# Delta rule of a hybrid block on one core: k-k and q-k products with 256 columns at a time, strictly alternating heads, and a later turn of nbp

## The chip, the cores and the metric

The kernel runs on one core of a Trainium2 chip. A core has five engines that run at the same time, each through its own instructions in order: TensorE (PE; its weight loads are shown apart as PEld), VectorE (DVE), ScalarE (ACT), GpSimd (POOL) and SyncE (SP), which here issues nearly all DMAs. The metric is the device time in microseconds of one execution; lower is better.

## The reference, cut to what matters

One block of a hybrid network on 1024 tokens of width 1024, in float32: a dilated attention of 8 heads and a gated delta rule of 8 heads side by side, their joint output projection, then a gated feed-forward part. The change touches the delta rule, which works in chunks:

```
q = l2norm(q) / sqrt(64); k = l2norm(k)            # per head, 64 wide
gcum   = cumsum(g) within a chunk
a_mat  = strictly_lower((beta * k) @ k.T * exp(gcum_i - gcum_j))
sol    = solve(a_mat + I, [beta * v, beta * k * exp(gcum)])   # u and w
qk     = lower(q @ k.T * exp(gcum_i - gcum_j))
for each chunk:                                     # the scan over the state
    v_new = u - w @ state
    o     = (q * exp(gcum)) @ state + qk @ v_new
    state = state * exp(g_last) + (k * exp(g_last - gcum)).T @ v_new
```

So each head needs, for every chunk, the products k @ k.T and q @ k.T, both multiplied with the same table of decays.

## The kernel before, in words

The kernel takes chunks of 128 positions, eight of them. The eight delta heads are worked through in two groups g of four heads (`delta(0)`, `delta(1)`); within a group, heads go in pairs q = 0, 1, and a pair's two heads lie in one tile, one head in partitions 0 to 63 and the other in 64 to 127. `kd[hp]` and `qd[hp]` are the k and q of pair hp = 2g + q, transposed (64 rows for each head, 1024 positions), each a tile of its own in the pools' tags "kd" and "qd" with two buffers each.

`delta` first makes k and q of a group by convolution (`conv`, for the second group in `delta_early` with a detour through memory: the DMA of L1240 brings it back from `_.cv`), and turns them (`delta_turn`, L737) for their norms. Then `delta_prep` does this:

- It makes the norms rk, and from them nbp (L774), nbg, kds and lr.
- ScalarE turns the tables `lts[h]` (named dt in the trace) into decays, one exponential for each head h and position block n (L770), head after head.
- `nbp` is transposed on the PE (L780, bank `ps_bp`), copied out, and written to memory (`bp_d`, L783), from where `delta_rows_in` reads it back in another layout (`bpr`, L855) for the inverse.
- For each pair: four q-k products for each head into one PSUM bank, then the other four; then the same for k-k (L799, tiles `kk_q` and `kk_k`). A product has 64 rows and 128 columns. DVE multiplies each full bank of 512 columns with the decays (L805): q-k into the tiles `qk`, k-k in place into `lts`. The k-k results go to memory (`lt_d`, L812).
- POOL scales kt with kds and qd with its own decays (L824, L839).

After that `delta_rows_in` loads the k-k results (`nt`, L853); `delta_inverse` multiplies them with bpr (L888), inverts 32 x 32 blocks in 31 steps on DVE (L899, L903), sends the result through memory (`tn`, L908) and joins the blocks for each head with PE products (the first of them at L931). `delta_scan` runs over the chunks; its readout uses qd (L1045).

Banks: `sbank` and `tbank` hand out two PSUM banks each, `abank` one. A tile that uses a bank again waits until its last reader is done.

The PE's other work in this phase is the projections (`others`, written as a generator through `proj_d`, L590, and `proj_t`, L616; their weights are split into a high and a low part by ACT and POOL, one of them by DVE, L230 and L231). They are put between the products of the delta rule by hand: `turn(name)` takes as many microseconds of them as the table `FILL` says for that name, and orders the instructions inside it behind the last of them. `tc.issue_after(ins)` orders what is written inside it behind `ins` on the same engine. `until` and `hold` take other products until one of them is done; `hold` stands ahead of the inverse's PE products, with 4 us for the first group and 24 for the second. What is left is spread over the first units of attention (`attend`, `FRONT - used[0]`). Every 7.6 us of other products, `modulation` adds a burst of its own (L211). Where no order is given, the framework takes instructions by priority, mostly in the order of the program.

Of the kernel before, what the change touches and what calls it, by code (L numbers as in the profile page):

```python
# [18 lines left out]
P = 128  # L19
# [33 lines left out]
    "S0_0_0": 3.84,  # L53
    "S1_0_0": 5.12,
    "trv2_0": 12.8,
    "kk1_0_0_q": 6.4,
    "trq1_0False": 4.48,
    "trk1_0False": 1.92,
    "kk0_2_0_k": 1.28,
    "lc0_0": 1.92,  # L60
    "trq3_0False": 2.56,
    "et0_0_0": 1.92,
    "sy1_6": 1.92,
    "kk1_3_0_k": 0.64,
    "et5_5_4": 1.28,
    "y0_0": 0.64,
    "trv3_0": 10.24,
    "kk1_0_0_k": 0.64,
    "sb0_6": 1.92,
    "et7_4_4": 0.64,  # L70
    "et4_6_0": 0.64,
# [1 line left out]
    "S6_0_0": 0.64,  # L73
    "sy1_0": 0.64,
    "sy1_7": 0.64,
    "kk0_0_0_k": 0.64,
}
for step in "abcd":
    for h in range(4):
        FILL.setdefault(f"l{step}0_{h}", 0.64)  # L80


def build(tc, I, out):
# [69 lines left out]
    def tbank(name):  # L153
        return psb(name, "t", 2)

    def abank(name):
        return psb(name, "a", 1)
# [4 lines left out]
    def start(name, tag, shape=None, dt=F32):  # L162

        n = {"xp": 2, "qk": 4, "lu": 5, "o": 2, "VN": 2, "R": 1, "tc": TCB, "yt": 1, "os": 1, "zl": 1}.get(tag, 2)
        return (pr if tag in ("dt", "xp") else pd).tile(shape or [P, T], dt, name=name, tag=tag, bufs=n)
# [7 lines left out]

    rb = const([33, 8], "rb")
    nc.vector.memset(rb[32:33, :], 1.0)
    tbl = start("tbl", "qd", [33, T]), start("tbl2", "qd", [33, P])
    wa8 = start("wa8", "qk", [P, KT, P])
    for i in range(2):
        nc.sync.dma_start(wa8[:, 4 * i : 4 * i + 4], I["wa8"][:, 4 * i : 4 * i + 4])
# [11 lines left out]
    for j in range(3):  # L191
# [5 lines left out]
        Rs = start(f"Rs{j}", "tc", [8, HALF])  # L197
        nc.vector.tensor_scalar(out=Rs[:, 0:n], in0=ps[:8, 0:n], scalar1=-1.0, scalar2=None, op0=ALU.mult)
        Rss.append(Rs)
    sqs = [start(f"sq{i}", "qd") for i in range(2)]  # L200

    sh1 = const([P, KT + 31], "sh1")
    nc.vector.memset(sh1, 0.0)
# [51 lines left out]
    wf = [start(f"wf{j}", ("dt", "xp")[j // 2], [P, 2, HALF]) for j in range(3)]  # L255
    wf = [wf[k // 2][:, k % 2] for k in range(5)]
    wf += [wp.tile([P, WSLOT], F32, name=f"wf{k}", tag="wr", bufs=3)[:, 0:HALF] for k in range(5, 8)]
    xts = [start(f"xt{k}", "lu" if k < 5 else ("vb" if k < 7 else "kd")) for k in range(KT)]

    def x_load(k):  # L260
        nc.sync.dma_start(xts[k], I["xT"][k * P : (k + 1) * P])
# [53 lines left out]
            )  # L315

    V0 = 16
    vraw = [start(f"vraw{i}", ("kd", "kt")[i], [P, 2, HALF]) for i in range(2)]

    def v_load(s):  # L320
        for j in range(2):
# [234 lines left out]
            )  # L556
        nc.scalar.activation(dst, dst, AF.Silu)

    kd, qd = {}, {}
    last, taken = [None], [None]  # L560
    fill = [None]
    used = [0.0]
# [1 line left out]
    def ahead(us):  # L564
# [7 lines left out]
            used[0] += w  # L572
        return some and last[0] is not None

    @contextmanager
    def turn(name):

        with tc.issue_after(last[0].ins) if ahead(FILL.get(name, 0)) else ExitStack():
            yield


# [171 lines left out]
    def delta_prep(g, st, norms, kt, lts):  # L753

        rk, eq, nbp, nbg, kds, lr = (norms[k] for k in ("rk", "eq", "nbp", "nbg", "kds", "lr"))
        gs = slice(32 * g, 32 * g + 32)

        def g3(t):
            return t[:, gs].rearrange("p (n h) -> p n h", n=8)

        eqf = eq.rearrange("p n h -> p (n h)")

        if g == 1:
            nc.scalar.activation(lr, rk, AF.Ln, bias=eps1)
        nc.vector.tensor_scalar(out=lr, in0=lr, scalar1=-0.5, scalar2=None, op0=ALU.mult)
        nc.scalar.activation(rk, lr, AF.Exp)
        nc.vector.tensor_tensor(out=lr, in0=lr, in1=g3(Gc), op=ALU.subtract)
        for h in range(4):
            for n in range(8):
                nc.scalar.activation(lts[h][:, n], lts[h][:, n], AF.Exp, bias=lr[:, n, h : h + 1])  # L770
        nc.vector.tensor_scalar(
            out=eqf, in0=eqf, scalar1=EPS, scalar2=64 * EPS, op0=ALU.add, op1=ALU.mult
        )
        nc.vector.scalar_tensor_tensor(  # L774
            out=nbp, in0=g3(beta), scalar=-1.0, in1=rk, op0=ALU.mult, op1=ALU.mult
        )
        nc.vector.tensor_tensor(out=nbg, in0=nbp, in1=g3(eG), op=ALU.mult)
        nc.vector.tensor_tensor(out=kds, in0=rk, in1=g3(edec), op=ALU.mult)
        ps = tbank(f"ps_bp{g}")
        nc.tensor.transpose(ps[:32, 0:P], nbp.rearrange("p n h -> p (n h)"), ident)  # L780
        nbpT = pd.tile([32, P], F32, name=f"nbpT{g}", tag="nbpT", bufs=1)
        nc.vector.tensor_copy(nbpT, ps[:32, 0:P])
        nc.sync.dma_start(_.bp[g], nbpT)  # L783

        qks = []
        for q in range(2):
            hp = 2 * g + q
            two = [pd.tile([P, 8, P], F32, name=f"qk{g}_{2 * q + e}", tag="qk", bufs=4) for e in range(2)]
            qks += two
            for dsts, mov, wh in ((two, qd[hp], "q"), (lts[2 * q : 2 * q + 2], kd[hp], "k")):  # L790
                for hf in range(2):

                    ps = [(sbank, tbank)[hf](f"kk{g}_{2 * q + e}_{hf}_{wh}") for e in range(2)]
                    with turn(f"kk{g}_{2 * q}_{hf}_{wh}"):
                        for j in range(4):
                            n = 4 * hf + j
                            for e in range(2):
                                rows = slice(64 * e, 64 * e + 64)
                                nc.tensor.matmul(  # L799
                                    ps[e][:, j * P : (j + 1) * P], kd[hp][rows, n * P : (n + 1) * P],  # L800
                                    mov[rows, n * P : (n + 1) * P], start=True, stop=True,
                                )
                    ns = slice(4 * hf, 4 * hf + 4)
                    for e in range(2):
                        nc.vector.tensor_tensor(  # L805
                            out=dsts[e][:, ns], in0=ps[e].rearrange("p (n i) -> p n i", n=4),
                            in1=lts[2 * q + e][:, ns], op=ALU.mult,
                        )
            for e in range(2):
                lt = lts[2 * q + e]  # L810
                for b in range(4):
                    nc.sync.dma_start(  # L812
                        bass.AP(
                            tensor=_.lt[g].tensor,
                            offset=_.lt[g][0:1, :].offset + (2 * q + e) * 4096 + b * 1024,
                            ap=[[32, 32], [16384, 8], [1, 32]],
                        ),
                        lt[32 * b : 32 * b + 32, :, 32 * b : 32 * b + 32],
                    )

        for q in range(2):
            hp = 2 * g + q
            with tc.issue_after(sel[g].ins):
                nc.gpsimd.tensor_tensor(  # L824
                    out=kt[q].rearrange("p n (e d) -> p n e d", e=2),
                    in0=kt[q].rearrange("p n (e d) -> p n e d", e=2),
                    in1=bc(kds[:, :, 2 * q : 2 * q + 2], 64), op=ALU.mult,
                )
            eb = pr.tile([P, 8, P], F32, name=f"eb{hp}", tag="dt", bufs=2)
            for e in range(2):  # L830
                nc.sync.dma_start(
                    eb[64 * e : 64 * e + 64],
                    bass.AP(
                        tensor=_.G.tensor, offset=_.G[0:1, :].offset + (32 * g + 2 * q + e) * P,
                        ap=[[0, 64], [4 * P, 8], [1, P]],
                    ),
                )
            nc.scalar.activation(eb, eb, AF.Exp)
            nc.gpsimd.tensor_tensor(  # L839
                out=qd[hp], in0=qd[hp], in1=eb.rearrange("p n i -> p (n i)"), op=ALU.mult  # L840
            )
        st.update(nbp=nbp, nbg=nbg, eq=eq, kt=kt, lts=lts, qks=qks, gs=gs)
# [383 lines left out]
    def delta(g):  # L1226
        st = {}
        kt = []
        for j in range(4):
            kind, q = ("k", j) if j < 2 else ("q", j - 2)  # L1230
            hp = 2 * g + q
            t = pd.tile([P, T], F32, name=f"{kind}d{hp}", tag=f"{kind}d", bufs=2)
            (kd if kind == "k" else qd)[hp] = t
            if g == 0:
                conv((4 if kind == "k" else 0) + hp, xps[j], t)
                kt.append(delta_turn(g, kind, q, t, norms=norms[0], keep=kind == "k"))
                if j == 1:
                    nc.scalar.activation(norms[0]["lr"], norms[0]["rk"], AF.Ln, bias=eps1)
            else:
                nc.sync.dma_start(t, _.cv[j])  # L1240
                if kind == "k":
                    kt.append(delta_turn(g, kind, q, t, keep=True))
        delta_prep(g, st, norms[g], kt[0:2], delta_rows(g))
        rows = delta_rows_in(g, st)
        if g == 1:
            until(lambda: "vd" in done)
        delta_v(g, st, [lambda q=q: vxp[q] if g == 0 else fetch(4 + q, f"v{2 + q}") for q in range(2)], rows)
        delta_inverse(g, st)
        until(lambda: ("z0", "z1")[g] in done)
        delta_scan(g, st)  # L1250
        if g == 0:
            delta_early()
# [775 lines left out]
```

## Time and profile before

| | us |
|---|---|
| median of 3 runs | 1401.86 |
| the three runs | 1393.12, 1401.86, 1402.77 |
| span of the profiled execution, first to last instruction | 1389.5 |
| PE busy | 1343.3 (97% of the span) |
| DVE busy | 875.5 (63%) |
| ACT busy | 660.1 (48%) |
| POOL busy | 266.8 (19%) |

The three times are of whole executions; the profile gives no time of its own beyond the span, and the median is 12.4 us above the span. In rows of the profile, L799 is line 799 of the kernel, `kk_q<-qd,kd` names output and inputs without buffer numbers, `64*128 64x128` the weights' and the moving operand's shape, and an arrow with an engine names what ended the idle time before an instruction. One float32 product shows as two records on the PE.

### The profile page before, as it was taken

What the parts mean: (1) busy time and instruction counts of PE and PEld (TensorE: products, weight loads), DVE (VectorE), ACT (ScalarE), POOL (GpSimd) and SP (SyncE); (2) the same over time, 40 slices, a digit from 0 to 9 for tenths busy, and PEclk for the clock granted to TensorE, in tenths of its full rate; (3) what the DMA queues carried; (4) which work ended last, traced back from release to release, by engine and by line L of the source; (5) the groups of instructions that cost most, each with busy time, mean ns of one, the idle gap of its engine ahead of it and who ended that gap; (6) DMA issues with size and microseconds to landing.
All of it is one profiled execution on the core that took longest, in us unless ns stands there. A gap on an engine that the chain in (4) does not pass through costs nothing.

```text
span 1389.5 us, 24383 instructions
## 1 busy us (share of the span) xinstructions
PE 1343.3 (97%) x8984; PEld 1106.9 (80%) x8984; DVE 875.5 (63%) x1678; ACT 660.1 (48%) x1285; POOL 266.8 (19%) x250
## 2 busy tenths in 40 slices
PE   8998999999999999899999999999999999999998
PEld 4777887888889877678777788888888888888876
DVE  3687583657846242766258977666675776474497
ACT  4497514347233454775168533333333333444455
POOL 2345303324213433543261000000000000000000
PEclk9999899999999999999999999999999999999999
DMA  8666574476362546522675346444453665765585
GB/s 311 228 194 168 160 213 156 138 235 156 124 165 80 172 134 182 153 91 70 217 230 174 124 143 211 140 156 168 152 174 124 213 209 186 255 222 193 191 270 192
DMA packets 169871, 245.64 MB, mean 177 GB/s; under 512 B 32566, under 2 KB 73831, under 8 KB 169752
## 3 DMA queue, kind: packets, MB, share of 16 engines
q1 hardware_dynamic: 169752, 244.08, 54.4%
q8 instruction: 71, 1.16, 0.3%
q14 instruction: 48, 0.39, 0.1%
HBM read 181.27 MB, written 67.48 MB: 179 GB/s over the span
## 4 chain that ended last, share of the span: by engine, by line
PE 71%; DVE 14%; DMA 5%; ACT 4%; issue 3%; POOL 2%; SPq 0%; POOLq 0%; DVEq 0%; ACTq 0%
PE wua L1622 9%; PE wga L1622 8%; PE X L1822 6%; PE wuc L1622 4%; PE wgc L1622 4%; PE g_a L590 4%; PE wo L590 3%; PE Z L1822 3%; PE y L1373 2%; PE wub L1622 2%; PE wgb L1622 2%; PE Y L1822 2%; DVE tm L899 2%; PE g_va L616 2%; PE f L251 2%
## 5 line engine op out<-in xcount | busy, mean ns | idle before, releaser
L1612 DVE TENSOR_TENSOR wl_db<-wr_db,wh_db 128x512 fp32r<-128x512 f32 x77 | 52.8, 689 | 66.4 <-ACT wh_db L1611 66.4
L1611 ACT CAST wh_db<-wr_db 128x512 fp32r<-128x512 f32 x77 | 47.6, 621 | 86.3 <-PE X L1822 37.8
L1332 DVE CUSTOM_DVE_ANT_0 X<-S,ng 128x512 f32<-128x512 f32 (+3 forms) x64 | 36.6, 587 | 62.7 <-PE S L1329 54.7
L1339 POOL TENSOR_SCALAR X<-X,sc 128x128 f32<-128x128 f32 (+7 forms) x64 | 48.9, 767 | 90.4 <-DVE sc L1338 77.5
L1822 PE MATMUL X<-wl_db,wh_da 128*128 128x512 f32 x160 | 62.4, 390 | 0.3 <-DVE wl_db L1612 0.3
L1337 ACT ACTIVATE X<-X,sc 128x128 f32<-128x128 f32 (+7 forms) x64 | 49.4, 773 | 27.8 <-DVE sc L1332 26.3
L1822 PE MATMUL X<-wh_db,wl_da 128*128 128x512 f32 x160 | 62.3, 389 | 0.0
L1822 PE MATMUL X<-wh_db,wh_da 128*128 128x512 f32 x160 | 62.2, 389 | 0.0
L1612 DVE TENSOR_TENSOR wl_da<-wr_da,wh_da 128x512 fp32r<-128x512 f32 x77 | 52.8, 686 | 4.0 <-ACT wh_da L1611 4.0
L1611 ACT CAST wh_da<-wr_da 128x512 fp32r<-128x512 f32 x77 | 47.5, 617 | 14.2 <-DMA wr_da<-ao_d 7.8
L590 PE MATMUL wo<-yh,wh_wo 128*128 128x512 f32 x128 | 51.9, 406 | 0.0
L590 PE MATMUL g_a<-hh,wh_a 128*128 128x512 f32 x128 | 51.4, 401 | 0.0
L590 PE MATMUL wo<-yh,wl_wo 128*128 128x512 f32 x128 | 51.2, 400 | 0.0
L590 PE MATMUL wo<-yl,wh_wo 128*128 128x512 f32 x128 | 50.5, 395 | 0.5 <-DVE yl L1440 0.5
L590 PE MATMUL g_a<-hl,wh_a 128*128 128x512 f32 x128 | 50.7, 396 | 0.0
L590 PE MATMUL g_a<-hh,wl_a 128*128 128x512 f32 x128 | 50.4, 394 | 0.0
L1352 PE MATMUL tr<-ident,X 128*128 128x128 f32 x288 | 44.1, 277 | 4.7 <-ACT et L1357 2.3
L1611 ACT CAST wh_wg_s<-wg_s 128x512 fp32r<-128x512 f32 x33 | 20.5, 622 | 58.6 <-PE wuc L1622 24.8
L1352 PEld LDWEIGHTS tr<-ident,X 128*128 128x128 f32 x288 | 32.6, 140 | 15.9 <-POOL X L1339 7.2
L1611 ACT CAST wh_wu_s<-wu_s 128x512 fp32r<-128x512 f32 x33 | 20.4, 622 | 45.0 <-PE wga L1622 17.2
L1611 ACT CAST wh_wg<-wr_wg 128x512 fp32r<-128x512 f32 x31 | 19.3, 621 | 46.8 <-PE wua L1622 19.2
L231 POOL TENSOR_TENSOR wl_wo<-wr_wo,wh_wo 128x512 fp32r<-128x512 f32 x24 | 31.9, 1333 | 47.3 <-ACT wh_wo L230 43.1
(554 smaller groups left out, 4345.1 us busy)
## 6 DMA issues: line engine op xcount, KB each, us to landing
wm<-in_wada SPq DMA_DIRECT2D x44, 512.0 KB, 6.7
wr_da<-ao_d SPq DMA_DIRECT2D x77, 256.0 KB, 3.0
wr_wu<-in_wu SPq DMA_DIRECT2D x50, 256.0 KB, 2.8
wr_wg<-in_wg SPq DMA_DIRECT2D x48, 256.0 KB, 3.0
ao_d<-a SPq DMA_DIRECT2D x44, 256.0 KB, 2.5
wr_wd<-in_wdn SPq DMA_DIRECT2D x44, 256.0 KB, 3.0
wr_db<-wt_d SPq DMA_DIRECT2D x44, 256.0 KB, 3.0
ao_d<-as SPq DMA_DIRECT2D x33, 256.0 KB, 2.1
```

What stands on the lines that cost most here:

```text
L231: (eng or nc.gpsimd).tensor_tensor(out=lo[:, :n], in0=raw[:, :n], in1=hi[:, :n].bitcast(F32), op=ALU.subtract)
L251: nc.tensor.matmul(first[bank], a[:, w0], b[k][:, cs], start=(k == 0 and n_ == 0), stop=(k == KT - 1 and n_ == 2))
L590: last[0] = nc.tensor.matmul(ps, a[:, w0], b[k0 + k4][:, cs], start=(i == 0), stop=(i == n - 1))
L616: last[0] = nc.tensor.matmul(ps[:, :n], a[k][:, ts_], b[:, w0], start=(i == 0), stop=(i == 23))
L1332: nc.vector.tensor_tensor_reduce(out=X[:, c0:c1], in0=ps[:, 0 : c1 - c0], in1=ng[:, u + c0 : u + c1], scale=1.0, scalar=(3e38 if m is None ...
L1337: nc.scalar.activation(X[:, 0:nk], X[:, 0:nk], AF.Exp, scale=-1.0, bias=m, accum_out=sc[:, 2:3])
L1339: nc.gpsimd.tensor_scalar(out=X[:, 0:nk], in0=X[:, 0:nk], scalar1=sc[:, 3:4], scalar2=0.0, op0=ALU.mult, op1=ALU.add)
L1352: nc.tensor.transpose(ps[:, (kb - c0) * P : (kb - c0 + 1) * P], X[:, kb * P : kb * P + P], ident)
L1611: nc.scalar.copy(hi, src)
L1612: (eng or nc.vector).tensor_tensor(out=lo, in0=src, in1=hi.bitcast(F32), op=ALU.subtract)
L1622: nc.tensor.matmul(ps, a[:, w0], b, start=(first and k == 0 and n_ == 0), stop=(k == 3 and n_ == 2), skip_group_check=True,)
L1822: nc.tensor.matmul(bank[b], a[:, ts_], w, start=(first and n_ == 0), stop=(last and n_ == 2), skip_group_check=True,)
```

## The change

The k and q of a pair now lie in one tile `kq[hp]` with two halves (k in the first, q in the second; tag "kq", two buffers, in place of "kd" and "qd"), and the tiles that used those buffers at the start of the kernel are halves of the same two buffers. One matmul takes 256 columns: the same weights, k of one head and block, against k and q of that block. A pair is worked through in four steps c of two blocks; the two heads alternate, each matmul ordered behind the one before it, and other products stand only between the steps: 0.64 us ahead of each, 5.12 and 6.4 us ahead of the first of each group. DVE reads 256 columns at a time, first q-k, then k-k. The exponentials of ACT go block by block within a pair. The transpose of nbp, its copy and its store come behind the second step of the first pair, in the bank of `abank`.

```diff
     "trv2_0": 12.8,
-    "kk1_0_0_q": 6.4,
+    "kk1_0_0": 6.4,
+    "kk0_0_0": 5.12,
...
-    "kk0_2_0_k": 1.28,
...
-    "kk1_3_0_k": 0.64,
...
-    "kk1_0_0_k": 0.64,
...
-    "kk0_0_0_k": 0.64,
 }
+for g in range(2):
+    for c in range(8):
+        FILL.setdefault(f"kk{g}_{c // 4 * 2}_{c % 4}", 0.64)
...
-    tbl = start("tbl", "qd", [33, T]), start("tbl2", "qd", [33, P])
+    two = [start(f"two{i}", "kq", [P, 2, T]) for i in range(2)]
+    tbl = two[0][0:33, 0, :], two[1][0:33, 0, 0:P]
...
-    sqs = [start(f"sq{i}", "qd") for i in range(2)]
+    sqs = [two[i][:, 0] for i in range(2)]
...
-    xts = [start(f"xt{k}", "lu" if k < 5 else ("vb" if k < 7 else "kd")) for k in range(KT)]
+    xts = [start(f"xt{k}", "lu" if k < 5 else "vb") for k in range(KT - 1)] + [two[1][:, 1]]
...
-    vraw = [start(f"vraw{i}", ("kd", "kt")[i], [P, 2, HALF]) for i in range(2)]
+    vraw = [two[0][:, 1].rearrange("p (j n) -> p j n", j=2), start("vraw1", "kt", [P, 2, HALF])]
...
+    def behind_(ins):
+        return tc.issue_after(ins.ins) if ins else ExitStack()
+
     @contextmanager
-    def turn(name):
-
-        with tc.issue_after(last[0].ins) if ahead(FILL.get(name, 0)) else ExitStack():
+    def turn(name, after=None):
+
+        with behind_(after):
+            some = ahead(FILL.get(name, 0))
+        with behind_(last[0] if some else after):
             yield
...
-        for h in range(4):
+        for q in range(2):
             for n in range(8):
-                nc.scalar.activation(lts[h][:, n], lts[h][:, n], AF.Exp, bias=lr[:, n, h : h + 1])
+                for h in (2 * q, 2 * q + 1):
+                    nc.scalar.activation(lts[h][:, n], lts[h][:, n], AF.Exp, bias=lr[:, n, h : h + 1])
...
-        ps = tbank(f"ps_bp{g}")
-        nc.tensor.transpose(ps[:32, 0:P], nbp.rearrange("p n h -> p (n h)"), ident)
-        nbpT = pd.tile([32, P], F32, name=f"nbpT{g}", tag="nbpT", bufs=1)
-        nc.vector.tensor_copy(nbpT, ps[:32, 0:P])
-        nc.sync.dma_start(_.bp[g], nbpT)
+
+        def betas():
+            ps = abank(f"ps_bp{g}")
+            nc.tensor.transpose(ps[:32, 0:P], nbp.rearrange("p n h -> p (n h)"), ident)
+            nbpT = pd.tile([32, P], F32, name=f"nbpT{g}", tag="nbpT", bufs=1)
+            nc.vector.tensor_copy(nbpT, ps[:32, 0:P])
+            nc.sync.dma_start(_.bp[g], nbpT)
 
         qks = []
+        mm = None
         for q in range(2):
...
-            for dsts, mov, wh in ((two, qd[hp], "q"), (lts[2 * q : 2 * q + 2], kd[hp], "k")):
-                for hf in range(2):
...
+            for c in range(4):
+
+                ps = [(sbank, tbank)[c % 2](f"kk{g}_{2 * q + e}_{c}") for e in range(2)]
+                ps = [t.rearrange("p (j w i) -> p j w i", j=2, w=2) for t in ps]
+                with turn(f"kk{g}_{2 * q}_{c}", mm):
+                    for j in range(2):
+                        n = 2 * c + j
+                        for e in range(2):
+                            rows = slice(64 * e, 64 * e + 64)
+                            with behind_(mm if j + e else None):
+                                mm = nc.tensor.matmul(
+                                    ps[e][:, j], kd[hp][rows, n * P : (n + 1) * P],
+                                    kq[hp][rows, :, n * P : (n + 1) * P], start=True, stop=True,
                                 )
+                ns = slice(2 * c, 2 * c + 2)
+                for w in (1, 0):
                     for e in range(2):
+                        lt = lts[2 * q + e]
                         nc.vector.tensor_tensor(
+                            out=(lt, two[e])[w][:, ns], in0=ps[e][:, :, w], in1=lt[:, ns], op=ALU.mult,
                         )
+                if (q, c) == (0, 1):
+                    with behind_(mm):
+                        betas()
...
-            t = pd.tile([P, T], F32, name=f"{kind}d{hp}", tag=f"{kind}d", bufs=2)
+            if kind == "k":
+                kq[hp] = pd.tile([P, 2, T], F32, name=f"kq{hp}", tag="kq", bufs=2)
+            t = kq[hp][:, kind == "q"]
             (kd if kind == "k" else qd)[hp] = t
```

More of the change, by code (lines that the diff above doesn't have):

```diff
@@ L557, in conv @@
         nc.scalar.activation(dst, dst, AF.Silu)
-    kd, qd = {}, {}
+    kd, qd, kq = {}, {}, {}
     last, taken = [None], [None]
@@ L789, in delta_prep @@
             qks += two
-            for dsts, mov, wh in ((two, qd[hp], "q"), (lts[2 * q : 2 * q + 2], kd[hp], "k")):
-                for hf in range(2):
[L793 to L801, printed above, removed]
-                                )
-                    ns = slice(4 * hf, 4 * hf + 4)
+            for c in range(4):
[10 more added lines that the diff above has]
+                                    kq[hp][rows, :, n * P : (n + 1) * P], start=True, stop=True,
+                                )
+                ns = slice(2 * c, 2 * c + 2)
+                for w in (1, 0):
                     for e in range(2):
+                        lt = lts[2 * q + e]
                         nc.vector.tensor_tensor(
-                            out=dsts[e][:, ns], in0=ps[e].rearrange("p (n i) -> p n i", n=4),
-                            in1=lts[2 * q + e][:, ns], op=ALU.mult,
-                        )
+                            out=(lt, two[e])[w][:, ns], in0=ps[e][:, :, w], in1=lt[:, ns], op=ALU.mult,
+                        )
+                if (q, c) == (0, 1):
+                    with behind_(mm):
+                        betas()
             for e in range(2):
```

## The prediction

> **What bounds the kernel now.** I read the page first: its head, the busy times and the row of granted clock over 40 slices.
>
> ```profile
> span 1389.5 us, 24383 instructions
> PE 1343.3 (97%) x8984; PEld 1106.9 (80%) x8984; DVE 875.5 (63%) x1678; ACT 660.1 (48%) x1285; POOL 266.8 (19%) x250
> PEclk9999899999999999999999999999999999999999
> ```
>
> TensorE (PE) sets the time: it is busy 97% of the span, so PE time taken out is worth about its own length, if nothing else then becomes late. Its clock is full except in the fifth slice (139 to 174 us), where the first group's k-k and q-k products run. So I read the stretches around those products, with busy time, instruction counts and granted clock (PEclk), and then the line of these products.
>
> ```profile
> core 0: us, PE busy (x) PEld busy (x) DVE busy (x) ACT busy (x) POOL busy (x), PEclk, DMA share, GB/s
> 132.36:134.46 2.10, 0.00 (x1) 0.01 (x1) 2.10 (x6) 0.16 (x1) 0.00 (x0) 1.00 0.73 217
> 136.00:145.70 9.70, 9.70 (x73) 9.70 (x74) 6.62 (x10) 9.70 (x32) 2.37 (x2) 0.50 0.66 153
> 145.70:149.59 3.89, 3.74 (x52) 3.24 (x49) 3.63 (x7) 3.30 (x4) 3.80 (x2) 0.96 0.35 55
> 317.47:329.59 12.12, 11.57 (x133) 10.15 (x132) 8.92 (x14) 12.05 (x36) 4.71 (x3) 1.00 0.77 174
> ...
> L799 PE MATMUL kk_q<-qd,kd x128: 271/272/578, 134.7 to 326.7; 64*128 64x128 f32 x128
> L799 PE MATMUL kk_k<-kd x128: 272/272/579, 138.8 to 329.4; 64*128 64x128 f32 x128
> ```
>
> Each of the 128 products (64 q-k, 64 k-k) is two records of 64 rows by 128 columns. In the first group the PE stands still for 2.10 us, then runs these products until 149.59, and for 9.70 us of that at clock 0.50, although it is never idle there. 73 records took those 9.70 us (0.133 us each), while in the next 3.89 us 52 records ran (0.075 us each) at 0.96. What differs is which rows are in use: in the slow stretch the records are mostly one head's, whose 64 rows are half of the array; where both heads' records start together the clock is back. The second group runs at 1.00 throughout, but partly head by head too. Who ended the 2.10 us is in the waits:
>
> ```profile
> PE ps_bp L780 <- DVE nbp L774: 2.1, 1, 2.1
> ```
>
> It is the transpose of nbp, which stands ahead of the products in program order.
>
> **The change part by part.** *Products.* Strictly alternating heads run as pairs, one on each half of the rows. What a pair costs, and what it costs to enter and leave these products, I take from the second group:
>
> ```profile
> 316.94 0.60 PE L737 MATMUL trk_0True<-ident,kd 128*128 128x128 f32 x4
> 317.47 0.49 PE L799 MATMUL kk_q<-qd,kd 64*128 64x128 f32 x4
> 317.89 0.66 PE L737 MATMUL trk_1True<-ident,kd 128*128 128x128 f32 x4
> ...
> 328.83 0.83 PE L799 MATMUL kk_k<-kd 64*128 64x128 f32 x10
> 329.59 0.39 PE L616 MATMUL g_va<-wh_va,hl 128*128 128x256 f32 x1
> ```
>
> Ten records span 0.83 us; less one record's own 0.27 us that is 0.56 us for five pair steps, so 0.112 us per step of 128 columns and about 0.22 for 256. A chunk of the new loop (two positions, two heads, four matmuls, eight records) is four such steps: 0.88 us. Entering: the four trk records start over 0.60 - 0.27 = 0.33 us (0.11 apart), so the last starts at 317.27 and the next product 0.20 later, 0.09 more than that step. The four kk_q records, two pairs, take 0.49 - 0.27 = 0.22 us between the pairs, 0.10 more than a paired step. Leaving, the last product starts at 317.69 and the next trk at 317.89, again 0.09 late. Together 0.28 us a chunk, if other products stand around each: 1.16 us. With 16 chunks, 18.6 us.
>
> [...]
>
> Today the two groups hold the PE for 149.59 - 132.36 = 17.23 us, less 0.21 for the transpose itself (134.46 to the first product at 134.67), which stays, so 17.02, and for 12.12 us less 0.59 for the four trk transposes in between (0.66 less the last record's 0.27, plus 0.20 to the next product), so 11.53: 28.55 us. The difference, **28.55 - 18.6 = 9.9 us**, is the gain: 7.7 of it in the first group (17.02 - 9.3) and 2.2 in the second. This counts on the 2.10 us of waiting and the half clock both going away: the first chunk now has 5.12 us of other products ahead of it, which start where the PE now stands still (132.36), and the transpose comes behind the second chunk.
>
> *Other products between.* They are only moved. FILL gave the two groups 9.0 us (6.4, 1.28 and twice 0.64; the key kk1_3_0_k matches no turn) and gives them now 5.12 + 6.4 + 14 x 0.64 = 20.5; the rest, 11.5 us, is missing later, where it is no loss as long as the PE stays busy. *Evictions.* 32 of 512 elements become 64 of 256.
>
> ```profile
> L433 DVE TENSOR_TENSOR bat<-sums,rr 128x256 f32<-128x256 f32 x1 | 0.4, 379 | 0.0
> L1068 DVE TENSOR_TENSOR o<-o,zl 128x256 f32<-128x256 f32 x16 | 7.5, 470 | 5.2 <-DMA zl<-zg_d 4.9
> L770 ACT ACTIVATE dt<-dt,lr 128x128 f32<-128x128 f32 x32 | 9.5, 388 | 0.0
> ...
> 328.37 1.28 DVE L805 TENSOR_TENSOR dt<-kk_k,dt 128x512 f32<-128x512 f32 x2
> 330.62 1.52 DVE L553 SCALAR_TENSOR_TENSOR vd<-xp_v,cw,vd 128x1023 f32<-128x1023 f32 x1 [0.97 <-ACT vd L551]
> 332.06 0.68 DVE L805 TENSOR_TENSOR dt<-kk_k,dt 128x512 f32<-128x512 f32 x1
> 332.66 2.27 DVE L231 TENSOR_TENSOR wl_z<-wr_z,wh_z 128x512 fp32r<-128x512 f32 x1
> 334.86 0.68 DVE L805 TENSOR_TENSOR dt<-kk_k,dt 128x512 f32<-128x512 f32 x1
> ```
>
> Back to back, one of 512 takes 1.28 - 0.68 = 0.60 us; one of 256 is 0.30 us shorter by the first row (0.38 against 0.68), so 0.30 to 0.39 apart by the two 256 rows. Four per chunk are 1.2 to 1.6 us, under the PE's 1.16 + 0.64 = 1.80 with its share of other work: hidden. With that cover gone VectorE (DVE) would cost up to 16 x (1.56 - 1.16) = 6.4 us. ScalarE's (ACT) 32 exponentials, now position by position within a pair, take 9.5 us a group, 1.2 per chunk: hidden by the same 1.80.
>
> *Turn of nbp, and the shared kq buffers.* Rows for both:
>
> ```profile
> 135.83 0.34 SPq L783 DMA_DIRECT2D bp_d<-nbpT  x1
> 172.12 1.86 DVE L888 TENSOR_TENSOR nt<-nt,bpr 128x1024 f32<-128x1024 f32 x1 [12.71 <-DMA nt<-lt_d]
> L1240 SPq DMA_DIRECT2D kd<-cv_d x2: 320/368/417, 282.6 to 285.0; - x2
> L1045 PE MATMUL o<-S,qd x6: 270/275/328, 281.2 to 285.8; 128*128 128x128 f32 x6
> L737 PE MATMUL trk_0True<-ident,kd x8: 272/273/328, 314.9 to 317.3; 128*128 128x128 f32 x8
> ```
>
> The store bp_d moves from 135.83 to about 142; behind it on SP's queue stand spill stores and the lt stores, which wait for evictions of that time anyway, and its reader runs at 172. Cost 0, up to 6 us only if the weight loads behind it were late. The second group's two k loads must now wait for the first group's last q readout (285.8) as well, not only for its last k product: some 3 us later on SP, ahead of a first use at 314.9. Cost 0. The start-up tiles pair the same lifetimes as before: 0.
>
> *What is late next.* The PE reaches the inverse's first products (L931) earlier; they need tn.
>
> ```profile
> 207.66 1.78 DVE L936 STREAM_TRANSPOSE U<-tn 32x256 f32<-32x256 f32 x4 [0.25 <-DMA tn<-tn_d]
> 219.35 0.69 PE L931 MATMUL lv<-tn,dt 32*32 32x32 f32 x32
> PE lv L931 <- DMA tn<-tn_d: 0.6, 1, 0.6
> 152.98 0.46 SPq L812 DMA_DIRECT2D lt_d<-dt  x1
> 157.27 0.35 SPq L229 DMA_DIRECT2D wr_z<-in_wz  x1
> 157.71 1.87 SPq L812 DMA_DIRECT2D lt_d<-dt  x4
> ```
>
> In the first group tn is there at 207.66 and the PE comes at 219.35: 11.7 us of slack, of which 7.7 are used and 4.0 left. In the second the PE already waits 0.6 us for tn; there FILL puts 3.8 us more between (10.9 against 7.0), and 2.2 are saved, so it arrives 1.6 later than now counted from the group's start: 2.2 us of slack. Both hold.
>
> **Sum.** 1389.5 - 9.9 = 1379.6 us of span. What lies around the span I take as 1401.9 (median) - 1389.5 = 12.4; the times do not say which run was profiled, and against the lowest one (1393.1) only 3.6 would lie around it. 1379.6 + 12.4 = **1392.0 us**, 0.7% below the median.
>
> **The rivals.** *The clock stays low* (the change does not do what it says). For it: clock 0.50 held 9.7 us with the PE never idle. Against: 0.96 once pairs ran, 1.00 in the second group. The first group's eight chunks then take 8 x 0.88 = 7.0 us more: a gain of 2.9, 1399 us. Chance 0.10.
>
> *DVE pieces between the evictions hand part back.* For it: DVE already puts a convolution and a weight split of 1.5 and 2.3 us before the last two evictions (332.06, 334.86); among the chunks, the strict order would make the PE wait for their banks with all that stands behind. Such a pair in each group is 3.8 us, less the room of four chunks (1.80 - 1.40 each, 1.6): 2.2 a group, 4.4 in all, 1396 us. Against: now no such piece stands among the first six of the group's eight k evictions. Chance 0.20.
>
> *Both chains to the inverse come late* (slower). The lt stores sit in SP's queue behind weight loads that wait for a free slot: 152.98 + 0.46 to 157.27 is 3.8 us of it now, and with more products used in the stage the loads have other places. If each chain, counted from its group's start, comes z later, the PE waits z - 4.0 and z - 2.2; that equals 9.9 at z = 8.0. At z = 10 it waits 13.8: 1406 us, and if each wait is followed by a stretch at half clock as the 2.10 us one was (9.70 us, so 4.85 lost), up to 1416. Against: the first pair's lt stores can go earlier, since its evictions no longer wait for the other head's exponentials. Chance 0.12.
>
> *The full pairing gain.* Chunks flow into their neighbours without the 0.28 us: 14.5 us, 1387 us. For it: part of the entry cost may hide in weight loads that are half as many; against: all three rows show it. Chance 0.11.
>
> **How the numbers follow.** My forecast has 0.47, with its own range 1388 to 1396 (the chunk at 1.0 to 1.4 us). The range for 8 in 10 reaches to the full pairing gain plus the 3 us that the place of the profiled run leaves open, 1384, and to where late chains have taken the gain and a little more, 1404. A measurement of this kernel can tell about 1% from no change: the three runs differ by 0.7%. Faster by over 1% means under 1387.8: most of the last rival and a tail, 0.12. Slower by over 1% means above 1415.9: the late chains with the low clock and what I do not see, 0.07. Within 1%: 0.81.
>
> **What would show it.** Right: no wait for nbp; PEclk at 0.95 or more in every stretch of the first group's products; 128 product records of 256 columns with pair starts 0.22 us apart and chunks 1.0 to 1.3 us of PE; the L931 products of the first group 7 to 8 us earlier and those of the second 6 to 8 earlier, with under 1 us of waiting for tn. Wrong: a granted clock near 0.50 there; PE waits for DVE evictions between chunks of over 0.3 us on the mean; or PE waits for tn of several us, in which case the gain of the stage is visible and the end does not move.

## The result, and the profile after

The changed kernel takes 1410.17 us (median of 6 runs, 1409.06 to 1411.78), the kernel before 1396.26 us in the same comparison (1392.98 to 1402.77): a ratio of 1.0108 (95% interval 1.0083 to 1.0134). The forecast was 1392.0 us. The profiled execution has a span of 1408.6 us against 1389.5: 19.1 us more, where the medians differ by 13.9. The mean granted clock of a kernel differs from run to run in this case, and the time follows it (the kernel before took 1392.1 us at 0.996 and 1411.9 at 0.977), so single times below are read together with the clock of their profile.

Head, busy row and granted clock of the page after:

```profile
span 1408.6 us, 24191 instructions
PE 1347.8 (96%) x8856; PEld 1101.9 (78%) x8856; DVE 877.3 (62%) x1710; ACT 662.1 (47%) x1286; POOL 269.1 (19%) x250
PEclk9998999978999999999999999999999999999999
```

The PE is busy 4.5 us longer, though 128 records are gone; the other 14.6 of the 19.1 us are idle time. There is a new low stretch in slices nine and ten (282 to 352 us). Four stretches of the kernel after, with busy time and count of each engine, granted clock, DMA share and GB/s:

```profile
127.13:134.96 7.83, 1.83 (x9) 1.43 (x9) 7.50 (x11) 4.66 (x7) 5.77 (x4) 0.65 0.60 187
134.96:155.40 20.44, 20.25 (x119) 12.04 (x120) 13.19 (x35) 14.96 (x40) 5.80 (x3) 0.80 0.57 126
...
296.60:323.90 27.30, 11.88 (x51) 9.01 (x50) 18.34 (x24) 19.09 (x29) 5.35 (x4) 0.57 0.67 208
323.90:339.60 15.70, 15.70 (x112) 11.32 (x113) 10.21 (x29) 13.05 (x34) 5.17 (x3) 0.99 0.37 75
```

and the same stretch ahead of the second group's products in the kernel before:

```profile
296.03:317.47 21.44, 20.91 (x212) 18.77 (x211) 14.78 (x24) 17.26 (x29) 6.18 (x5) 1.00 0.86 280
```

This is most of the loss. The first PE product of the inverse (tile lv) starts 2.7 us late in the first group (222.0 us against 219.3) and 21.0 us late in the second (408.0 against 387.0). Ahead of the second group's products stand the convolutions of its q rows and eight squared norms, work of DVE and ACT. Before, 212 PE records ran there, 100 of them products of va and 64 of modulation; after, 51 run, the PE is idle 15.4 of 27.3 us, and what it does run goes at a clock of 0.57. What it waited for (window 110 to 326 us):

```profile
PE trq_0False L743 <- ACT cv L558: 10.5, 2, 5.4
PE yt L1093 <- DVE o L1083: 4.8, 4, 3.0
PE kk L810 <- ACT sqq L749: 4.0, 2, 3.8
...
PE trq_0False L743 <- ACT kq L558: 2.2, 1, 2.2
```

The 10.5 us of waiting for cv were 0.5 us before, in the same window:

```profile
PE trq_0False L737 <- ACT cv L557: 0.5, 1, 0.5
```

The kernel after, in order of time:

```profile
296.34 0.28 PE L622 MATMUL g_va<-wl_va,hh 128*128 128x256 f32 x1
299.62 0.41 PE L1093 MATMUL yt<-ident,o 128*128 128x128 f32 x2 [3.01 <-DVE o L1083]
...
309.94 1.11 PE L743 MATMUL trq_0False<-ident,cv 128*128 128x128 f32 x4 [5.44 <-ACT cv L558]
...
317.00 1.11 PE L743 MATMUL trq_0False<-ident,cv 128*128 128x128 f32 x4 [5.10 <-ACT cv L558]
...
323.93 1.87 PE L810 MATMUL kk<-kq 64*128 64x256 f32 x8
325.73 0.39 PE L622 MATMUL g_va<-wh_va,hh 128*128 128x256 f32 x1
```

From 296.34 to 325.73 no product of va stands anywhere; the next comes behind the first chunk. The cause can be read in the diff: `turn(name, after=mm)` queues each share of 0.64 us behind the last k-k matmul. The products come out of one generator and use two banks in turn, so the first queued share holds every later product. In the kernel before none was queued, and they slipped forward into any wait.

### The profile page after: what moved, and what is told of

The parts are those of the page before. It is cut to its first block, busy times and chain, and to the rows that moved or that the text cites. A ratio compares the mean times of both kernels' runs of the same rounds, so it can differ in the third digit from the quotient of the medians.

```text
span 1408.6 us, 24191 instructions
## 1 busy us (share of the span) xinstructions
PE 1347.8 (96%) x8856; PEld 1101.9 (78%) x8856; DVE 877.3 (62%) x1710; ACT 662.1 (47%) x1286; POOL 269.1 (19%) x250
## 4 chain that ended last, share of the span: by engine, by line
PE 77%; DVE 9%; DMA 5%; ACT 4%; issue 3%; POOL 2%; SPq 0%; POOLq 0%; DVEq 0%; ACTq 0%
PE wua L1639 9%; PE wga L1639 8%; PE X L1839 6%; PE g_a L596 5%; PE wgc L1639 4%; PE wuc L1639 4%; PE wo L596 4%; PE g_va L622 3%; PE g_z L622 3%; PE Z L1839 3%; PE wub L1639 2%; PE wgb L1639 2%; PE Y L1839 2%; PE y L1390 2%; PE f L252 2%
```

## The experiments

**The first theory: queued shares dry the PE out.** Rivals: the shared kq buffers, the later turn of nbp, the strict order itself.

*float* takes the queue off the shares only:

```diff
-        with behind_(after):
-            some = ahead(FILL.get(name, 0))
-        with behind_(last[0] if some else after):
+        some = ahead(FILL.get(name, 0))
+        with behind_(last[0] if some else None), behind_(after):
```

> The changed kernel, but the 0.64 shares of other products are no longer queued behind the last kk product; the kk products keep their strict order. Theory (the queued shares hold all later products back, so the PE runs dry in the conv chains): the products float forward again, the PE's idle time between 290 and 325 us falls from about 17 us to under 4, and most of the 17.8 us lost there come back; the chunks then stand back to back and wait for their four evictions (4 x 0.33 = 1.3 us against 0.88), some 0.4 us a chunk. 1392 to 1398 us. Rivals (shared kq buffers and later loads, the later turn of nbp, the strict order itself): the waits for the convolved rows stay uncovered, 1405 to 1412 us.

*float_g1* does so in the second group alone:

```diff
-        with behind_(after):
+        with behind_(None if name.startswith("kk1") else after):
```

> As the run before, but the shares float in the second group only. Theory: the 17.8 us are lost in the second group and 2.6 in the first, so this gives back nearly all: 1391 to 1397 us, with the first group's two waits before the products (2.2 and 3.8 us) and its low clock unchanged. Rival (the loss comes from the first group's low clock and is only carried along): 1404 to 1411.

*cover* keeps the queue and traces more products where nothing queues them:

```diff
-    "trv2_0": 12.8,
-    "kk1_0_0": 6.4,
-    "kk0_0_0": 5.12,
+    "trv2_0": 0.64,
+    "kk1_0_0": 19.2,
+    "kk0_0_0": 7.04,
```

> The changed kernel with the queued shares kept, but more products traced ahead of the first kk product of each group, where nothing queues them (19.2 us instead of 6.4 in the second group, 7.04 instead of 5.12 in the first; the 12.8 us ahead of trv2 become 0.64). Theory: free products fill the waits again and the chunks keep their cover, so the prediction's gain of up to 9.9 us appears: 1384 to 1391 us. Rivals (buffers, nbp, strict order): 1403 to 1412, since none of them is touched.

*nbp_early* puts the transpose of nbp and its store ahead of the products again, in the old bank:

```diff
-                if (q, c) == (0, 1):
-                    with behind_(mm):
-                        betas()
+        ps = tbank(f"ps_bp{g}")
+        nc.tensor.transpose(ps[:32, 0:P], nbp.rearrange("p n h -> p (n h)"), ident)
...
```

> The changed kernel with the transpose of nbp and its store ahead of the products again, as before the change. Theory: nothing comes back, 1407 to 1413 us. Rival (the later turn of nbp is what costs): 5 us or more come back, 1405 or less.

Measured (in brackets the ratio to the kernel before in the same comparison, and its 95% interval): float 1411.72 us (1.0096, 1.0060 to 1.0131), float_g1 1412.13 (1.0095, 1.0058 to 1.0131), cover 1415.94 (1.0151, 1.0113 to 1.0189), nbp_early 1415.16 (1.0141, 1.0096 to 1.0186). The turn of nbp is not it. For the other three the times lie with the rivals or above them, but the profiles do not fit these: the stretch is filled again, in float (first row), in cover (second) and in float_g1 (PE busy 32.4 of the 35 us).

```profile
290.00:325.00 35.00, 32.23 (x301) 29.51 (x302) 18.57 (x34) 25.47 (x50) 11.19 (x8) 1.00 0.87 260
```
```profile
290.00:325.00 35.00, 30.92 (x309) 27.33 (x302) 18.00 (x33) 24.25 (x47) 10.52 (x9) 1.00 0.85 254
```

The queue does dry the PE out, then, and yet taking it off gives nothing measurable back: the theory as a whole had fallen. The loss had moved. The first lv product of the second group now starts at 390.7 us in float and at 396.7 in cover instead of 408.0, but behind a wait for tn, and the stretch from 390 to 440 us runs at a low clock (float's two rows, then cover's):

```profile
390.00:440.00 50.00, 47.98 (x680) 42.06 (x681) 19.45 (x54) 14.29 (x36) 5.40 (x7) 0.66 0.36 98
...
PE lv L945 <- DMA tn<-tn_d: 3.9, 1, 3.9
```
```profile
390.00:440.00 50.00, 42.61 (x686) 37.16 (x687) 19.37 (x54) 15.04 (x38) 5.97 (x8) 0.76 0.47 120
...
PE lv L946 <- DMA tn<-tn_d: 7.4, 1, 7.4
```

Not every run of float pays this: three of its ten took 1395.9 to 1400.2 us, the others 1408.3 to 1415.2; the profiled one took 1411.9.

**The second theory: the chain to tn takes over.** PE work saved ahead of the inverse becomes a wait for tn, and the clock falls behind it. One line outside the diff stands behind that: `hold(*LEVELS[g])` runs products ahead of the inverse up to a fixed mark, with `LEVELS = ("z0", 4), ("z1", 24)`, that is, until z1 is done and 24 us of products more.

*cover_lv* and *float_lv* add products there:

```diff
-LEVELS = ("z0", 4), ("z1", 24)
+LEVELS = ("z0", 4), ("z1", 32)
```

(30 in float_lv.)

> The run cover, with 8 us more of other products traced ahead of the second group's inverse (32 instead of 24 us after the last z1 product). The first theory has fallen: in cover the waits of the convolutions are filled (PE idle between 290 and 325 us 3 us instead of 17) and the time is still above before. New theory: the second group's first inverse products (lv) wait for tn, which a chain of VectorE, stores and loads delivers; PE time saved before it becomes a wait (7.4 us in cover), and after the wait the clock stays at half through the inverse's small products (390 to 415 us). With the wait filled by real products both go: the clock is 1.00 there and the time 1396 to 1404 us. Rival (the evictions of 256 columns and the strict order cost by themselves, the wait only shows it): the 8 us of products are 8 us late, 1414 to 1422 us.

> The run float, with 6 us more of other products ahead of the second group's inverse (30 instead of 24). In float lv waited 3.9 us for tn and the clock fell to half for some 35 us after it. New theory: no wait, clock 1.00 between 385 and 440 us, 1391 to 1399 us, at best what the chain to tn allows. Rival (the low clock has another cause than the wait): the clock is low there again, 1410 to 1418 us.

*before_light* tests the prediction's premise by itself, in the kernel before:

```diff
                 for a, b in ((hh, wh), (hl, wh), (hh, wl)):
+                    if name == "z1" and a is hl:
+                        i += 1
+                        continue
```

> The kernel before the change, with one of the three terms left out of the z1 products (hl times wh), which stand between the second group's products and its inverse: 6.8 us less PE work (64 products of 0.107 us), nothing else touched. The prediction's premise (PE time taken out is worth its length): 6.8 us faster, 1386 to 1390 us. New theory: lv comes no earlier than 387, it waits some 7 us for tn, and the low clock after that wait costs more: 1396 to 1408 us.

*before_alt* chains the old 128-column matmuls so that the two heads alternate:

```diff
+                                with tc.issue_after(mm.ins) if mm else ExitStack():
-                                nc.tensor.matmul(
+                                    mm = nc.tensor.matmul(
```

> The kernel before, with one part of the change alone: the k-k and q-k products of 128 columns queued so that the two heads of a pair strictly alternate. New theory: the half clock in the first group's products goes (9.7 us at 0.50 before), the stage is 4 to 6 us shorter, and the end hardly moves, since tn sets it: 1393 to 1408 us. Rival (the strict order is what costs 15 us by itself): 1406 to 1412 with PE waits between the products of the two groups.

Measured: cover_lv 1400.05 us (1.0019, 0.9996 to 1.0041), float_lv 1396.69 (1.0002, 0.9983 to 1.0020), before_light 1412.27 (1.0112, 1.0068 to 1.0157, of four runs), before_alt 1397.85 (1.0000, 0.9966 to 1.0033). The same 50 us, in float_lv and then in cover_lv:

```profile
390.00:440.00 50.00, 48.35 (x803) 43.22 (x801) 26.92 (x79) 19.64 (x49) 9.07 (x12) 1.00 0.50 133
```
```profile
390.00:440.00 50.00, 47.46 (x795) 42.59 (x794) 21.90 (x64) 17.54 (x44) 7.22 (x9) 1.00 0.56 149
```

With 6 or 8 us of products added, 15 to 16 us come back by the medians, 13 and 18 by the ratios. And before_light, with 64 products less (6.8 us by the kernel's own count; in the kernel before their starts lie 0.118 us apart from 340.74 to 341.92 us, which makes 7.6) and nothing else touched, is not 6.8 us faster: its four runs took 1395.5, 1407.8, 1416.8 and 1416.8 us. Its expectation was wrong in the place: in its profile, which is of the shortest run, the PE waits for tn no longer than before (0.6 us), since earlier waits grew instead (window 280 to 445 us):

```profile
PE g_z L619 <- ACT zt L640: 3.8, 1, 3.8
PE trv L878 <- ACT vd L557: 2.8, 2, 1.7
PE g_z L619 <- DVE wl_z L231: 2.3, 1, 2.3
PE lv L934 <- DMA tn<-tn_d: 0.6, 1, 0.6
```

The first three rows are other engines' work that the PE now comes too early for; they were 0.3, 1.3 and 1.4 us before. Besides, 6.8 us from 350.9 on run at a clock of 0.50, where the kernel before has 1.00. The premise falls all the same, as far as four runs can tell: the first lv product starts at 387.5 us, where it was 387.0 with the 64 products.

**Four runs to close the cross.** *after_lv*: the changed kernel with 32 in that line. *before_lv* and *before_alt_lv*: 26 in it. *float_short* leaves out the last 8 of 31 elimination steps of the second group:

```diff
-        for j in range(31):
+        for j in range(31 if g == 0 else 23):
```

> The changed kernel with 32 instead of 24 us of products ahead of the second group's inverse, and nothing else: the queued shares stay. Theory in two steps: in the changed kernel itself the loss is the dry PE in the convolutions (17 us idle and half clock between 296 and 325 us), and at lv it doesn't wait, so this addition alone gives nothing back: 1409 to 1419 us. Rival (one and the same wait for tn in all variants, so more products ahead of lv always cure it): 1396 to 1404 us, as in cover_lv.

> The kernel before, with 26 instead of 24 us of products ahead of the second group's inverse. The wait of 0.6 us for tn goes, the PE comes 1.4 us later than tn. Theory: nothing to gain on the mean but the runs in which the clock falls there; 1391 to 1397 us, ratio 0.996 to 1.001. A control for the next run.

> Strict alternation alone at 128 columns (before_alt), with 26 instead of 24 us ahead of the inverse. In before_alt the k-k and q-k products took 20.2 us of PE time instead of 26.0, lv came at 385.3 instead of 387.0, but the PE waited 1.2 us for tn and the clock then stayed at half for 45 us. Theory: the wait filled, the clock stays up and the 1.7 us of the chain are what is left of the gain: 1389 to 1395 us, ratio 0.994 to 0.999. Rival (the low clock has another cause): as before_alt, 1397 us with a wide spread.

> The run float with the last 8 of the 31 elimination steps of the second group left out, so that tn is there some 8 us earlier; the PE's work is the same. Theory (the chain over VectorE to tn sets when lv begins, and the wait of 3.9 us brings the clock down): lv begins at 386 to 387 without a wait, clock 1.00 after it, 1390 to 1397 us. Rival (the 256-column products or their evictions cost the time elsewhere): 1405 to 1412 us.

| shares | 24 us ahead of the inverse | 30 or 32 us |
|---|---|---|
| queued (the change) | 1410.17 (1.0108) | after_lv 1412.73 (1.0118, 1.0068 to 1.0169) |
| queued, more products ahead (cover) | 1415.94 (1.0151) | 1400.05 (1.0019) |
| floating | 1411.72 (1.0096) | 1396.69 (1.0002) |

Neither remedy gives anything measurable alone, both together give the loss back to within what can be told: two losses, one hidden behind the other. float_short, where the load of tn is out by 378.3 instead of 385.7 us, needs no added products: 1392.95 us (0.9973, 0.9944 to 1.0003), lv from 385.4 without a wait. So the chain over DVE to tn is what the PE meets there. before_lv takes 1391.43 us (0.9976, 0.9948 to 1.0003), before_alt_lv 1393.96 (0.9988, 0.9956 to 1.0021): no difference that can be told, and no gain for the alternation when its wait is filled.

**What float_lv still lacks.** In its profile the second group's products begin at 324.8 us, 7 later than before. (They begin 4 us later, at 321.6, in before_lv too, which takes no longer: a late start need not cost.)

*kq_lv*: the kernel before with the change's buffers alone, and 26 in the line above:

```diff
-            t = pd.tile([P, T], F32, name=f"{kind}d{hp}", tag=f"{kind}d", bufs=2)
+            if kind == "k":
+                kq[hp] = pd.tile([P, 2, T], F32, name=f"kq{hp}", tag="kq", bufs=2)
+            t = kq[hp][:, kind == "q"]
```

> The kernel before with the shared kq buffers alone (products of 128 columns, old order, nbp early), and 26 us of products ahead of the second group's inverse. In float_lv the second group's products begin 5 to 7 us later than before the change (324.8 against 317.5), and ACT loads a table more in the convolutions there (the exponential of rk comes ahead of the last silu). Theory: the shared buffers, whose k loads come later, change that order; the products begin 3 us or more later than in before_lv's order would put them, with four table loads between 305 and 318 us, 1392 to 1398 us. Rival (the order of the exponentials or the 256 columns do it): three table loads, as before.

*float_silu_lv*: float with 27 in the line above, and the exponential queued; *float_silu_lv30* the same with 30:

```diff
-        nc.scalar.activation(rk, lr, AF.Exp)
+        with behind_(silu[0] if g else None):
+            nc.scalar.activation(rk, lr, AF.Exp)
```

> The run float with 27 us of products ahead of the second group's inverse, and the second group's first exponential (rk) queued behind the last silu of the convolutions, as it stood before the change. Theory: a table load of 1.28 us less ahead of the products, they begin 2 to 3 us earlier than in float_lv, tn is there 2 to 3 us earlier, 1389 to 1395 us against 1396.7 for float_lv. Rival (what float_lv still lacks is lost in the evictions of 256 columns): 1395 to 1399 us.

> As float_silu_lv, with 30 us of products ahead of the second group's inverse instead of 27 (float_lv had 30). float_silu_lv, whose chain to tn is 4 us earlier than float_lv's, spread from 1395 to 1412 us with mean clocks of 0.983 to 0.996, while float_lv stayed within 1394 to 1402. Theory: the margin by which the PE comes after tn decides whether the clock falls in a run; with 30 it stays up: 1392 to 1399 us, narrow. Rival (the exponential's new place costs in most runs by itself): 1400 to 1410 us, as wide as with 27.

Table loads on ACT ahead of the second group's products, in kq_lv and then in the kernel before:

```profile
308.43 1.28 ACT L765 ACT_TABLE_LOAD   x1
310.55 1.28 ACT L767 ACT_TABLE_LOAD   x1
312.35 1.28 ACT L558 ACT_TABLE_LOAD   x1
315.21 1.28 ACT L771 ACT_TABLE_LOAD   x1
```
```profile
306.50 1.28 ACT L764 ACT_TABLE_LOAD   x1
308.62 1.28 ACT L557 ACT_TABLE_LOAD   x1
311.75 1.28 ACT L766 ACT_TABLE_LOAD   x1
```

The buffers alone bring the fourth load, as expected, but not the delay: kq_lv's products begin at 316.5, and it takes 1395.11 us (0.9991, 0.9966 to 1.0016). Putting the order back brings the products forward to 317.8 and tn from 387.0 to 382.6, but the time is worse: 1404.29 (1.0055, 1.0019 to 1.0091), and 1400.73 with 30 (1.0009, 0.9979 to 1.0040). This third theory fell. Its profile, a run at clock 0.996 and 1393.1 us of span, does not show why the other runs had mean clocks down to 0.983; that stays open. No version was measurably faster than the kernel before.

## Why the prediction was wrong, step by step

*The chunk: right within its range.* 1.16 us were forecast, with 1.0 to 1.4 allowed. Once the clock is full (1.00 from 143.40 to 155.40 us), a chunk's eight records span 1.13 us with other products around them:

```profile
139.95 2.08 PE L810 MATMUL kk<-kq 64*128 64x256 f32 x8
...
143.40 1.13 PE L810 MATMUL kk<-kq 64*128 64x256 f32 x8
144.46 0.50 PE L596 MATMUL g_kd<-hh,wh_kd 128*128 128x512 f32 x1
144.80 0.40 PE L596 MATMUL g_kd<-hl,wh_kd 128*128 128x512 f32 x1
145.03 0.40 PE L596 MATMUL g_kd<-hh,wl_kd 128*128 128x512 f32 x1
145.36 1.13 PE L810 MATMUL kk<-kq 64*128 64x256 f32 x8
```

That span holds the last record's own length and leaves out the way in and out. Counted as the forecast counts, it is 1.96 us from one chunk to the next, less 0.69 for the three products of the share (0.23 each, as from 144.80 to 145.03): 1.27 us, or 1.8 us more than forecast for the 16 chunks.

*"This counts on the 2.10 us of waiting and the half clock both going away": wrong.* The cover of 5.12 us slipped forward to other places, so at 127.13 the PE stood still for 2.2 us and then for 3.8 (waits above, kq and sqq), and the first chunks ran at half clock (0.50 from 134.96 to 142.00 us; the second one 2.08 us, first row above). The saving in PE busy time of the products is the difference of these busy times, in the windows 130 to 160 and 310 to 345 us (before, after, before_alt):

```profile
130.00:160.00 30.00, 14.84 (x128) 14.26 (x128) 0.83 0.56 140
310.00:345.00 35.00, 11.12 (x128) 9.73 (x128) 1.00 0.62 168
```
```profile
130.00:160.00 30.00, 12.17 (x64) 7.00 (x64) 0.78 0.57 141
310.00:345.00 35.00, 9.81 (x64) 5.84 (x64) 0.80 0.59 167
```
```profile
130.00:160.00 30.00, 10.30 (x128) 8.73 (x128) 0.94 0.60 148
310.00:345.00 35.00, 9.79 (x128) 8.29 (x128) 1.00 0.64 170
```

26.0 - 22.0 = 4.0 us, where 9.9 with the wait, 7.8 without it, were forecast. Alternation of the old 128-column products alone saves 26.0 - 20.1 = 5.9 us, 4.5 of it in the first group, where the clock of the window is 0.94 instead of 0.83 (0.94 in float, too, 0.78 in the changed kernel): with the heads strictly alternating and no queued share between them, most of the half clock does go. In the second group it takes as long as the change (9.79 and 9.81 us). The first group's inverse, forecast 7 to 8 us earlier, starts 2.7 us later (in float, without the queue, at 219.6 us, as before).

*Other products "are only moved ... no loss as long as the PE stays busy": the step that failed.* The sum priced a share by its own length. It left out that `behind_(after)` turns free work into queued work, and that what is queued also holds back all that comes behind it. The kernel before filled 10 us of waiting for cv with it. Queued, it fills nothing: the 15.4 idle us and the transposes at half clock (0.51 and 0.50 in the two 10 us from 300 us on), and an inverse that starts 21.0 us late. The shares also stretch the second group's products from 12.1 to 15.7 us, and the chain behind them gets later on SP:

```profile
341.28 4.80 SPq L827 DMA_DIRECT2D lt_d<-dt  x8
350.66 1.62 SPq L230 DMA_DIRECT2D wr_a<-in_wd  x2
...
352.94 0.33 SPq L868 DMA_DIRECT2D nt<-lt_d  x1
```

The load of nt stands behind weight loads that waited for their slot (5.3 us until POOL was done with wl_z, between 338 and 356 us); it goes out at 352.9 instead of 341.7. This is the mechanism of the third rival, one step further down the queue than it was put; here it cost nothing, since tn was loaded from 398.1 us on and the PE came to it at 408.0.

*The gates ("there FILL puts 3.8 us more between"): wrong.* The line of LEVELS tops the products up to the same mark whatever FILL gave earlier. Before and after, up to the first lv of the second group (287 and 308 us from 100 on), the records are the same in number:

```profile
L616 PE MATMUL g_z<-wh_z,hh 128*128 128x256 f32 x128 | 36.7, 287 | 2.2 <-ACT zt L637 2.2
L616 PE MATMUL g_va<-wh_va,hh 128*128 128x256 f32 x77 | 22.8, 296 | 0.0
```
```profile
L622 PE MATMUL g_z<-wh_z,hh 128*128 128x256 f32 x128 | 37.5, 293 | 3.5 <-ACT zt L643 3.5
L622 PE MATMUL g_va<-wh_va,hh 128*128 128x256 f32 x77 | 23.4, 304 | 0.0
```

So there was no slack of 2.2 us. Counted from the start of the products, as the forecast counts, the PE in float reaches lv 4.2 us earlier than before (64.7 us instead of 68.9), the load of tn goes out only 0.7 earlier (63.2 instead of 63.9), and the PE waits 3.9 us. Seen from the start of the kernel the PE comes no earlier at all (386.9 against 386.4): the products themselves begin 4.7 us later (322.2 against 317.5), and tn is late with them.

*"PE time taken out is worth about its own length": wrong* in this stretch: before_light takes 64 products out and gains nothing. A PE that is 97% busy with work that was put there to fill waits isn't a bound.

*Evictions and nbp: right.* The evictions are hidden where shares stand between the chunks; in float, without shares, they set a chunk's 1.33 us (four of them, 0.33 us apart without a gap; 10.68 us of PE for the second group's eight). No run shows a cost of the later nbp. The buffers change ACT's order but not the time.

*The rivals.* Slower by 1.08% was inside the third rival's bracket of 1406 to 1416 us, given 0.12, but its path was another: in the changed kernel the PE never waits for tn. *The 12.4 us around the span: wrong, too;* the profiled runs show about 2 (cover: 1410.66 against a span of 1408.5). Made with that, the same sum would have said 1381.7.

## What to carry to other kernels

Before ordering filler work "between" steps, ask what it fills today: free filler covers waits that no plan names, and one queued piece stops the whole stream behind it. Before pricing PE time at its own length, look for a mark that fixes how much filler stands ahead of the next gate: then a saving ahead of the gate can turn into a wait at it, or ahead of it, unless filler is brought forward as well. When undoing one part changes nothing, compare the profiles and not only the times: a second loss can stand right behind the first, and a cross of two remedies can show it.

## What the runs showed of the hardware that was not expected

In some runs a short wait was followed by a long stretch at half clock, which costs far more than the wait. In the profiled run of before_alt (1408.8 us, the slowest of ten; the median is 1397.9) 1.2 us of waiting for tn were followed by 50 us at a mean clock of 0.55, with the PE never idle (544 of its records ran there, 745 in the kernel before):

```profile
390.00:440.00 50.00, 50.00 (x544) 43.17 (x541) 16.07 (x46) 11.42 (x29) 5.75 (x8) 0.55 0.26 70
...
PE lv L933 <- DMA tn<-tn_d: 1.2, 1, 1.2
```

In the kernel before 0.6 us at the same place left the clock at 1.00. In float and cover the clock was 0.50 from 400 to 410 us, behind the 3.9 and 7.4 us of waiting for tn. In the changed kernel it was 1.00 in the 2.2 us of waiting from 127.13 us on and 0.55 in the 1.8 us behind them. In float_silu_lv the PE was idle for 2.8 us between 380 and 390 us, and the clock was 1.00 there and up to 440 us. So the length of a wait alone does not tell whether the clock falls behind it.

What keeps the clock low stays open. Few rows in use would fit the inverse's products of 32 and 64 rows, and the one head's 64 rows in the first group's slow stretch (0.50 from 136.00 to 145.70 us in the kernel before). But the inverse's products run at 1.00 in float_lv (390 to 440 us). In before_alt 116 records of modulation and 37 of va, all of 128 rows, ran in the low stretch too (387 to 435 us). And in float_short, with no wait at lv, the clock is 0.50 from 411.9 to 425.5 us with the PE never idle, while every record there uses 128 rows.
